# Three pairs by seven products for six units of the conv branch, in a decoder step on one core

## The chip, the cores and the metric

The kernel runs on one core of a Trainium2 chip. The metric is the time of the device in microseconds, median of several runs; lower is better. All matrix work is on TensorE in fp32r, with each operand split into a rounded part and its remainder, so that one product of fp32 accuracy is three matmuls (high by high, high by low, low by high).

## The reference

One layer of a decoder step over 1056 tokens (1024 of a prompt, 8 x 4 samples) of width 1024. The normed input h goes through one wide projection whose columns feed three branches and their gates:

```python
ua, va, q, k, v, cx, cb, cc, ga, gb, gc = split_proj(h, w_in)
out_a = gelu(ua) * spatial_gate(layer_norm(gelu(va)))
out_b = dilated_attention(q, k, v)            # prompt, and samples against a cache
conv, conv_state = short_conv(cc * cx, prev)  # y[t] = b + sum(w[i] * z[t - 2 + i], i = 0..2)
out_c = cb * conv
merged = sig(ga) * (out_a @ w_br_a) + sig(gb) * (out_b @ w_br_b) + sig(gc) * (out_c @ w_br_c)
x = x + rms_norm(merged @ w_o)                # then a SwiGLU block on the normed x
```

The conv branch is 512 wide: four tiles of 128 channels, and for each tile three column groups of w_in (cx, cb, cc), which are three "units".

## The kernel before

Everything lies with channels on the 128 partitions and tokens along the free dimension. A *unit* is 128 output columns of a weight, a tile of 128 x 1024 (eight blocks of 128 inputs). `unit(n)` (L161) takes the next unit of a fixed order written out in `_unit_order` (L47): SyncE's DMA queue loads it (`wr`), ScalarE rounds it (`wh`, L116), VectorE takes the remainder (`wl`, L117). Each of the three tags has three buffers, and one unit is prepared ahead. `fill` (L139) issues other loads on the same queue, behind the last weight load asked for.

**Two ways to multiply.** `proj` (L236) does a unit plainly: three blocks of 352 tokens, 24 matmuls each. `halved` and `seven` (L954, L1003) do two units at once with seven products on half matrices: weights and inputs are cut into halves, sums and differences of the halves are formed on VectorE, and each product is 4 x 3 matmuls of 264 columns for each of two sets of tokens. The first set is the first two quarters of 264 tokens, the second the last two. The differences of the input, kept as high and remainder in `sets`, are made by `halves` (L918) from quarters of h that were spilled to `h_dram`; each half set is four subtractions and four splits of 128 x 1056. `seven` uses four accumulators; with both sets each is a pair of banks (`pair`), with one set a single bank (`psum`).

**Order of the work around the change.** After the prompt's attention come the conv tiles f = 0 to 3 (L1056). For each: two units copied out by ScalarE to z and yb (L1063), a third multiplied into z by VectorE (L1071), in banks of the tag "mm", of which there are two. `conv` (L864) is a generator that then does the three taps on VectorE, multiplies by yb, and spills the result to `outs[6 + f]`. After each block `tick` steps two generators once: the taps of the last tile, and `attn`: the mix of the three dilation groups (L745), the four sample sets (L666, each loading 2.9 MB of masks, keys and values into six tiles, then scores, maximum, exp, transposes and values), and their sum (L812). After f = 2 `attn` is emptied and the first half set is begun; it is stepped during f = 3. Then two gate units are done plainly (L1097), with the second half set beside them, then eleven pairs of gate units by seven products (L1131), each spilled to `sig_dram`. Then the merges (L1167): for j = 0 to 7 three blocks of branch A, multiplied by a gate read back into a tile of V, and three of branch B; `branch_in` (L734) loads and splits the branches' outputs, and the ones of the conv branch come in during the first four steps; after that the merges of C.

Up to the plain gates a planner orders each engine's instructions by their order in the program and by when it thinks them ready; from the gates on (`as_written`, L1096) the matmuls keep the order of the program, and the rest is still planned. Tiles come from pools: 32 tiles of 128 x 1056 called U, of which h takes 16 and the two half sets 16 more, and three of the same size called V, until the merges end.

Of the kernel before, what the change touches and what calls it, by code (L numbers as in the profile page):

```python
# [8 lines left out]
F32 = mybir.dt.float32  # L9
F32R = mybir.dt.float32r  # L10
AF = mybir.ActivationFunctionType
ALU = mybir.AluOpType
AX = mybir.AxisListType

P = 128
# [4 lines left out]
T = TP + TS  # L20
# [25 lines left out]

def _unit_order():  # L47

    n = [(u, False) for u in range(U_G)]
    n[U_UA + 1] = (U_UA + 1, True)  # L50
    n += [(u, False) for u in (U_G, U_G + 1, )]
    n += [(U_BA, False), (U_BB, False), (U_BA + 1, False), (U_BA + 2, False), (U_BB + 1, False), (U_BA + 3, False)]
    n += [(u, False) for u in range(U_BC, U_BC + 4)]
    n += [(U_O + f, f >= REFETCH) for f in range(KD)]
    n += [(U_O + f, False) for f in range(REFETCH)] * 3
    return n
# [3 lines left out]
def tile_decoder_step(ctx: ExitStack, tc: tile.TileContext, i, o):  # L60
    nc = tc.nc
# [16 lines left out]
    def U(dt=F32, w=T):  # L78
        return up.tile([P, w], dt, tag="U", name=nm("U"))

    def V(dt=F32):

        return vp.tile([P, T], dt, tag="V", name=nm("V"))
# [4 lines left out]
    def psum(tag=None):  # L88

        if tag is None:  # L90
            turn[0] += 1
            tag = ("mm", "s", "s")[turn[0] % 3]
        return pp.tile([P, 512], F32, tag=tag, name=nm(tag), bufs=banks[tag])
# [13 lines left out]
    def tmp(tag="ta"):  # L107
        return small([P, 2 * QW], tag, 3)
# [46 lines left out]
    def ahead(n):  # L155
        while len(ready) < n and fetched[0] < len(order):
            m, spare = order[fetched[0]]
            ready.append((m, fetch(m, spare)))
            fetched[0] += 1

    def unit(n, more=1):  # L161

        ahead(1 + more)
        m, halves = ready.pop(0)
        assert m == n, (m, n)
        return halves

    def bs(b):
        return slice(b * BW, (b + 1) * BW)
# [564 lines left out]
    def branch_in(o0, nk, xs):  # L734

        ts = [U() for _ in range(nk)]
        for k, t in enumerate(ts):
            fill(t, outs[o0 + k])
        for t in ts:
            yield  # L740
            xs.append((U(F32R), U(F32R)))
            split(t, *xs[-1])
# [118 lines left out]
    cst = const("cst", [P, 4, 8, 2], i["cst"])  # L861
    convo = const("convo", [P, 4, 18])

    def conv(f, z, yb):  # L864

        zs = small([P, 8, 6], "zs")
        nc.vector.tensor_copy(zs[:, :, 0:2], cst[:, f])
        nc.vector.tensor_copy(zs[:, :, 2:6], z[:, TP:].rearrange("p (b t) -> p b t", t=4))
        nc.vector.tensor_copy(convo[:, f, 0:2], z[:, TP - 2 : TP])
        nc.vector.tensor_copy(convo[:, f, 2:18].rearrange("p (b t) -> p b t", t=2), zs[:, :, 4:6])  # L870
        yield
        y = V()
        cw = [vec(V_CW + 3 * f + t) for t in range(3)]
        cb_ = vec(V_CB + f)
        nc.vector.tensor_scalar(
            out=y[:, :TP], in0=z[:, :TP], scalar1=cw[2], scalar2=cb_, op0=ALU.mult, op1=ALU.add
        )
        ys = y[:, TP:].rearrange("p (b t) -> p b t", t=4)
        nc.vector.tensor_scalar(
            out=ys, in0=zs[:, :, 2:6], scalar1=cw[2], scalar2=cb_, op0=ALU.mult, op1=ALU.add  # L880
        )
        for s in (1, 2):
            nc.vector.scalar_tensor_tensor(
                out=y[:, s:TP], in0=z[:, : TP - s], scalar=cw[2 - s], in1=y[:, s:TP], op0=ALU.mult, op1=ALU.add
            )
            nc.vector.scalar_tensor_tensor(
                out=ys, in0=zs[:, :, 2 - s : 6 - s], scalar=cw[2 - s], in1=ys, op0=ALU.mult, op1=ALU.add
            )
            yield
        nc.vector.tensor_mul(y, y, yb)  # L890
        nc.scalar.dma_start(out=outs[6 + f], in_=y)
        if f == 3:
            nc.scalar.dma_start(out=o["conv"], in_=convo)
        yield

    attn = chain(mix_groups(), *(sample_set(se) for se in range(4)), sample_sum())
    taps = iter(())

    def tick():

        next(taps, None)
        next(attn, None)

# [12 lines left out]
    def halves(s, b11, b21, b12, b22):  # L918


        def sub(out, a, b):
            nc.vector.tensor_tensor(out=out, in0=a, in1=b, op=ALU.subtract)

        sub(b12, b12, b11)
        sub(b22, b22, b12)
        yield
        sub(b11, b22, b11)
        sub(b21, b21, b22)
        put(2, b22, s)
        yield  # L930
        put(3, b11, s)
        put(4, b12, s)
        yield
        put(5, b21, s)
        yield
# [10 lines left out]
    def pair():  # L946
        return pf.tile([P, 1024], F32, tag="pair", name=nm("pair"), bufs=4)
# [6 lines left out]
    def halved(n0, n1, spare):  # L954
# [29 lines left out]
        parts(6, r0[:, b], t, b)  # L984
        return out

    def banks_for(ss):
        return psum() if len(ss) == 1 else pair()

    def product(ps, w, n, ss, start=True):  # L990
        for e, s in enumerate(ss):
# [5 lines left out]
    def by_set(x, ss):  # L997

        return x.rearrange("p (s h t) -> p s h t", s=2, h=2)[:, ss[0] : ss[0] + len(ss)]
# [41 lines left out]
    def left(gen):  # L1041
        for _ in gen:
            pass

    def quarters(s):

        ts = []
        for q in (2 * s, 2 * s + 1):
            for c in range(2):
                t = (V if q == 2 and c else U)()  # L1050
                fill(t.rearrange("p (f t) -> p f t", f=4), h_dram[:, 4 * c : 4 * c + 4, qs_(q)])
                ts.append(t)
        return ts

    others = iter(())
    for f in range(4):  # L1056
        z, yb = U(), U()
        for q, dst in enumerate((z, yb)):
            w = unit(U_C + 3 * f + q)
            for b in range(NB):  # L1060
                ps = psum("mm")
                proj(w, b, ps)
                nc.scalar.copy(dst[:, bs(b)], ps[:, :BW])  # L1063
                tick()
                if f == 3:
                    next(others, None)
        w = unit(U_C + 3 * f + 2)
        for b in range(NB):
            ps = psum("mm")
            proj(w, b, ps)  # L1070
            nc.vector.tensor_tensor(out=z[:, bs(b)], in0=ps[:, :BW], in1=z[:, bs(b)], op=ALU.mult)  # L1071
            tick()
        left(taps)
        taps = conv(f, z, yb)
        if f == 2:
            left(attn)
            others = halves(0, *quarters(0))
    left(others)


    sig_dram = dp.tile([24, P, T], F32, tag="sig_dram", name="sig_dram")
# [13 lines left out]

    as_written[0] = True  # L1096
    for u in range(2):  # L1097
        sig, w = V(), unit(U_G + u)
        for b in range(NB):
            ps = psum()  # L1100
            proj(w, b, ps)
            sigmoid(sig[:, bs(b)], ps[:, :BW], u)
            if u == 0 and b == 0:
                left(taps)
                others = halves(1, *quarters(1))
            next(others, None)
        nc.scalar.dma_start(out=sig_dram[u], in_=sig)
    left(others)
    banked.close()
    mid = ExitStack()  # L1110
# [2 lines left out]
    def gates(w, u, ss, a0, a1):  # L1113
        v0, v1 = by_set(a0, ss), by_set(a1, ss)

        def add(out, ps, u2, u):
            nc.vector.tensor_tensor(out=out, in0=ps, in1=u2, op=ALU.add)
            sigmoid(out, out, u)

        def c22(t):  # L1120
            if t is not None:
                sigmoid(t, t, u + 1)
            return v1[:, :, 1]

        seven(
            w, ss, lambda ps: sigmoid(v0[:, :, 0], ps, u), c22,
            lambda ps, u2: add(v1[:, :, 0], ps, u2, u + 1),
            lambda ps, u2, t: add(v0[:, :, 1], ps, u2, u),
        )

    for u in range(2, 24, 2):  # L1131
        w = halved(U_G + u, U_G + u + 1, V)
# [16 lines left out]
    def merge(j, ts, sig, w, xs, first=False):  # L1149
        ps = psum()[:, : ts.stop - ts.start]  # L1150
        nk = len(xs)
        for k in range(nk):
            c = ((j % (KD // nk)) * nk + k) * P
            mm3(
                ps, (w[0][:, c : c + P], w[1][:, c : c + P]), (xs[k][0][:, ts], xs[k][1][:, ts]),
                k == 0, k == nk - 1,
            )
        dst, s = mg[j][:, ts], sig[:, ts]
        nc.vector.tensor_tensor(out=dst if first else s, in0=ps, in1=s, op=ALU.mult)
        if not first:  # L1160
            nc.vector.tensor_add(dst, dst, s)  # L1161

    xs_a, xs_b, xs_c = [], [], []
    coming = chain(branch_in(0, 4, xs_a), branch_in(4, 2, xs_b), branch_in(6, 4, xs_c))
    for _ in range(7):
        next(coming)
    for j in range(KD):  # L1167
        sig_a, sig_b = gated(j), gated(16 + j)
        if j % 2 == 0:
            wa = unit(U_BA + j // 2)  # L1170
        if j % 4 == 0:
            wb = unit(U_BB + j // 4)
        mg.append(U())
        for b in range(NB):
            merge(j, bs(b), sig_a, wa, xs_a, True)
        for b in range(NB):
            merge(j, bs(b), sig_b, wb, xs_b)
        next(coming, None)
    left(coming)

# [576 lines left out]
```

## Time and profile before

| | |
|---|---|
| median of 3 runs | 1662.18 us (1660.44 to 1662.22) |
| the profiled execution | 1661.68 us, its span 1660.0 us |
| TensorE matmul / weight load busy | 98% / 95% |
| VectorE / ScalarE busy | 62% / 37% |
| mean granted TensorE clock | 0.995 |
| DMA | 221 MB, 133 GB/s over the span |

Times in the rows below are microseconds from the span's start. A matmul's own duration overlaps its neighbours'; what one costs is read from the length of a run of them in the chain of work that ended last.

### The profile page before, as it was taken

What the parts mean: (1) busy time and instruction counts of PE and PEld (TensorE: products, weight loads), DVE (VectorE), ACT (ScalarE), POOL (GpSimd) and SP (SyncE); (2) the same over time, 40 slices, a digit from 0 to 9 for tenths busy, and PEclk for the clock granted to TensorE, in tenths of its full rate; (3) what the DMA queues carried; (4) which work ended last, traced back from release to release, by engine and by line L of the source; (5) the groups of instructions that cost most, each with busy time, mean ns of one, the idle gap of its engine ahead of it and who ended that gap; (6) DMA issues with size and microseconds to landing.
All of it is one profiled execution on the core that took longest, in us unless ns stands there. A gap on an engine that the chain in (4) does not pass through costs nothing.

```text
span 1660.0 us, 29423 instructions
## 1 busy us (share of the span) xinstructions
PE 1624.3 (98%) x12307; PEld 1572.3 (95%) x12307; DVE 1026.4 (62%) x1825; ACT 612.5 (37%) x1129; POOL 12.2 (1%) x23
## 2 busy tenths in 40 slices
PE   7999999999999999999999899999999999999997
PEld 6999887889899999999999899999999999999996
DVE  7536545563374445567776977666666667667586
ACT  7322234411133333341256663322232223344262
POOL 0000100000000000000000000000000000000000
PEclk9999999999999999999999999999999999999998
DMA  6332212033632222276464513333333336746571
GB/s 222 134 108 83 94 45 71 20 137 135 239 109 87 111 108 111 107 268 193 153 206 131 163 46 116 98 98 98 97 98 98 97 97 224 254 169 229 171 251 54
DMA packets 102684, 221.11 MB, mean 133 GB/s; under 512 B 13228, under 2 KB 59884, under 8 KB 102552
## 3 DMA queue, kind: packets, MB, share of 16 engines
q1 hardware_dynamic: 58256, 161.80, 29.5%
q10 hardware_dynamic: 44296, 57.44, 9.8%
q8 instruction: 96, 1.57, 0.4%
q14 instruction: 36, 0.29, 0.1%
HBM read 160.74 MB, written 58.47 MB: 132 GB/s over the span
## 4 chain that ended last, share of the span: by engine, by line
PE 91%; DVE 4%; DMA 2%; issue 1%; ACT 1%; SPq 0%; DVEq 0%
PE pair L123 36%; PE mm L123 19%; PE bank L123 13%; PE s L123 11%; PE s L603 2%; PE t L636 1%; PE o L581 1%; PE s L382 1%; PE s L384 1%; PE s L383 1%; DMA wr<-in_w 1%; DVE wl L117 1%; PE mm L382 1%; PE mm L384 1%; PE mm L383 1%
## 5 line engine op out<-in xcount | busy, mean ns | idle before, releaser
L123 PE MATMUL pair<-U,wh 128*128 128x264 f32 x2880 | 526.6, 284 | 1.6 <-DVE ta L1015 1.6
L123 PEld LDWEIGHTS pair<-U,wh 128*128 128x128 f32 x2880 | 445.7, 188 | 1.8 <-DVE ta L1015 1.8
L123 PE MATMUL pair<-U,wl 128*128 128x264 f32 x1440 | 408.4, 284 | 0.0
L116 ACT CAST wh<-wr 128x512 fp32r<-128x512 f32 (+1 forms) x264 | 192.3, 738 | 441.8 <-PE mm L123 164.7
L123 PE MATMUL mm<-U,wh 128*128 128x352 f32 (+1 forms) x1280 | 314.8, 325 | 2.7 <-ACT U L1063 2.0
L123 PEld LDWEIGHTS pair<-U,wl 128*128 128x128 f32 x1440 | 270.8, 188 | 0.0
L117 DVE TENSOR_TENSOR wl<-wr,wh 128x512 fp32r<-128x512 f32 (+1 forms) x264 | 216.5, 834 | 69.3 <-ACT wh L116 68.6
L123 PEld LDWEIGHTS mm<-U,wh 128*128 128x128 f32 x1280 | 219.5, 188 | 15.5 <-issue 8.8
L123 PE MATMUL bank<-U,wh 128*128 128x264 f32 x1232 | 226.2, 285 | 0.7 <-DVE U L1297 0.7
L123 PE MATMUL mm<-U,wl 128*128 128x352 f32 (+1 forms) x656 | 209.6, 320 | 0.0
L123 PE MATMUL s<-U,wh 128*128 128x352 f32 (+1 forms) x888 | 198.1, 310 | 8.0 <-ACT U L264 5.3
L123 PEld LDWEIGHTS bank<-U,wh 128*128 128x128 f32 x1232 | 191.2, 188 | 1.2 <-DVE U L1297 0.9
L123 PE MATMUL bank<-U,wl 128*128 128x264 f32 x616 | 175.1, 284 | 0.0
L123 PEld LDWEIGHTS s<-U,wh 128*128 128x128 f32 x888 | 149.1, 189 | 10.8 <-ACT U L264 5.3
L123 PE MATMUL s<-U,wl 128*128 128x352 f32 (+1 forms) x460 | 141.3, 307 | 0.0
L117 DVE TENSOR_TENSOR U<-U,U 128x1056 fp32r<-128x1056 f32 (+2 forms) x131 | 113.2, 886 | 23.6 <-ACT U L116 23.1
L123 PEld LDWEIGHTS mm<-U,wl 128*128 128x128 f32 x656 | 123.2, 188 | 1.7 <-issue 1.3
L116 ACT CAST U<-U 128x1056 fp32r<-128x1056 f32 (+2 forms) x131 | 100.1, 781 | 62.5 <-DVE U L1161 28.4
L123 PEld LDWEIGHTS bank<-U,wl 128*128 128x128 f32 x616 | 116.0, 188 | 0.0
L1015 DVE TENSOR_TENSOR tb<-pair,ta 128x528 f32<-128x528 f32 x49 | 34.7, 708 | 108.8 <-PE pair L123 108.8
L123 PEld LDWEIGHTS s<-U,wl 128*128 128x128 f32 x460 | 87.0, 189 | 0.0
L123 PE MATMUL pair<-U,U 128*128 128x264 f32 x456 | 58.5, 284 | 0.0
(291 smaller groups left out, 1863.4 us busy)
## 6 DMA issues: line engine op xcount, KB each, us to landing
wr<-in_w SPq DMA_DIRECT2D x121, 512.0 KB, 4.0
t_dram<-U ACTq DMA_DIRECT2D x77, 264.0 KB, 3.9
U<-t_dram SPq DMA_DIRECT2D x35, 528.0 KB, 5.8
sig_dram<-V ACTq DMA_DIRECT2D x24, 528.0 KB, 2.7
V<-sig_dram SPq DMA_DIRECT2D x24, 528.0 KB, 3.6
U<-in_kv SPq DMA_DIRECT2D x20, 512.0 KB, 6.7
wr<-in_wd SPq DMA_DIRECT2D x20, 512.0 KB, 4.3
U<-outs SPq DMA_DIRECT2D x10, 528.0 KB, 6.6
```

Of the source, the lines that this page charges most:

```text
L116: nc.scalar.copy(hi, x)
L117: (eng or nc.vector).tensor_tensor(out=lo, in0=x, in1=hi.bitcast(F32), op=ALU.subtract)
L123: ins = nc.tensor.matmul(*a, **k)
L382: nc.tensor.matmul(ps[:, :HV], h_hi[k][:, tk], wv[k][0], start=k == 0, stop=False)
L383: nc.tensor.matmul(ps[:, :HV], h_hi[k][:, tk], wv[k][1], start=False, stop=False)
L384: nc.tensor.matmul(ps[:, :HV], h_lo[k][:, tk], wv[k][0], start=False, stop=k == KD - 1)
L581: nc.tensor.matmul(po[0][h * 64 : (h + 1) * 64, (n % 4) * P : (n % 4 + 1) * P], vg[kb // 4][:, (kb % 4) * 256 + hd : (kb % 4) * 256 + hd + ...
L603: nc.tensor.matmul(ps, qT[hs_, n * P : (n + 1) * P], kg[hp][hs_, k0 : k0 + nk * P], start=True, stop=True,)
L636: last = nc.tensor.transpose(tp[:, at : at + P], pt[:, h, c * P : (c + 1) * P], ident)
L1015: nc.vector.tensor_tensor(out=out, in0=view(ps), in1=y, op=ALU.add)
```

## The change

Of the twelve conv units six stay plain: tiles f = 0 and 1. The generators of the attention are stepped three times per block for the first eight blocks and twice after. When the two tiles are done `attn` is emptied, and both half sets are stepped beside the two plain gates, together with the taps of tile 1. Then, before the eleven pairs of the gates, the six units of tiles 2 and 3 are done as three pairs by seven products: the first (cx of both tiles) with one set at a time but in pairs of banks, kept in two V tiles z; the second (cc) multiplied onto z as it comes out; the third (cb) into two V tiles yb. z and yb are spilled to a new `conv_dram`. In the merges' first steps `conv_late` reads them back to U tiles and does the taps of tiles 2 and 3, with the result in a U tile, and the second half of the conv branch's outputs is loaded four steps later than before. The first unit of branch A's weight is now prepared after the first pair and not before it.

```diff
@@ -46,7 +46,7 @@
 
 def _unit_order():
 
-    n = [(u, False) for u in range(U_G)]
+    n = [(u, False) for u in range(U_C + 6)]
     n[U_UA + 1] = (U_UA + 1, True)
     n += [(u, False) for u in (U_G, U_G + 1, )]
     n += [(U_BA, False), (U_BB, False), (U_BA + 1, False), (U_BA + 2, False), (U_BB + 1, False), (U_BA + 3, False)]
@@ -861,7 +861,7 @@
     cst = const("cst", [P, 4, 8, 2], i["cst"])
     convo = const("convo", [P, 4, 18])
 
-    def conv(f, z, yb):
+    def conv(f, z, yb, room):
 
         zs = small([P, 8, 6], "zs")
         nc.vector.tensor_copy(zs[:, :, 0:2], cst[:, f])
@@ -869,7 +869,7 @@
         nc.vector.tensor_copy(convo[:, f, 0:2], z[:, TP - 2 : TP])
         nc.vector.tensor_copy(convo[:, f, 2:18].rearrange("p (b t) -> p b t", t=2), zs[:, :, 4:6])
         yield
-        y = V()
+        y = room()
         cw = [vec(V_CW + 3 * f + t) for t in range(3)]
         cb_ = vec(V_CB + f)
         nc.vector.tensor_scalar(
@@ -896,10 +896,14 @@
     attn = chain(mix_groups(), *(sample_set(se) for se in range(4)), sample_sum())
     taps = iter(())
 
+    ticks = [0]
+
     def tick():
 
         next(taps, None)
-        next(attn, None)
+        ticks[0] += 1
+        for _ in range(3 if ticks[0] < 9 else 2):
+            next(attn, None)
 
 
 
@@ -984,8 +988,10 @@
         parts(6, r0[:, b], t, b)
         return out
 
+    paired = [False]
+
     def banks_for(ss):
-        return psum() if len(ss) == 1 else pair()
+        return psum() if len(ss) == 1 and not paired[0] else pair()
 
     def product(ps, w, n, ss, start=True):
         for e, s in enumerate(ss):
@@ -1052,8 +1058,10 @@
                 ts.append(t)
         return ts
 
-    others = iter(())
-    for f in range(4):
+    def second():
+        yield from halves(1, *quarters(1))
+
+    for f in range(2):
         z, yb = U(), U()
         for q, dst in enumerate((z, yb)):
             w = unit(U_C + 3 * f + q)
@@ -1062,8 +1070,6 @@
                 proj(w, b, ps)
                 nc.scalar.copy(dst[:, bs(b)], ps[:, :BW])
                 tick()
-                if f == 3:
-                    next(others, None)
         w = unit(U_C + 3 * f + 2)
         for b in range(NB):
             ps = psum("mm")
@@ -1071,11 +1077,9 @@
             nc.vector.tensor_tensor(out=z[:, bs(b)], in0=ps[:, :BW], in1=z[:, bs(b)], op=ALU.mult)
             tick()
         left(taps)
-        taps = conv(f, z, yb)
-        if f == 2:
-            left(attn)
-            others = halves(0, *quarters(0))
-    left(others)
+        taps = conv(f, z, yb, V)
+    left(attn)
+    others = chain(halves(0, *quarters(0)), second())
 
 
     sig_dram = dp.tile([24, P, T], F32, tag="sig_dram", name="sig_dram")
@@ -1095,16 +1099,17 @@
 
     as_written[0] = True
     for u in range(2):
-        sig, w = V(), unit(U_G + u)
+        sig, w = V(), unit(U_G + u, 1 - u)
         for b in range(NB):
             ps = psum()
             proj(w, b, ps)
             sigmoid(sig[:, bs(b)], ps[:, :BW], u)
-            if u == 0 and b == 0:
-                left(taps)
-                others = halves(1, *quarters(1))
+            left(taps)
             next(others, None)
+            if b:
+                next(others, None)
         nc.scalar.dma_start(out=sig_dram[u], in_=sig)
+    left(taps)
     left(others)
     banked.close()
     mid = ExitStack()
@@ -1127,6 +1132,57 @@
             lambda ps, u2: add(v1[:, :, 0], ps, u2, u + 1),
             lambda ps, u2, t: add(v0[:, :, 1], ps, u2, u),
         )
+
+    conv_dram = dp.tile([4, P, T], F32, tag="conv_dram", name="conv_dram")
+
+    def plain(w, ss, a0, a1):
+        v0, v1 = by_set(a0, ss), by_set(a1, ss)
+
+        def add(out, ps, u2):
+            nc.vector.tensor_tensor(out=out, in0=ps, in1=u2, op=ALU.add)
+
+        seven(
+            w, ss, lambda ps: nc.scalar.copy(v0[:, :, 0], ps), lambda t: v1[:, :, 1],
+            lambda ps, u2: add(v1[:, :, 0], ps, u2),
+            lambda ps, u2, t: add(v0[:, :, 1], ps, u2),
+        )
+
+    def times(w, ss, a0, a1):
+
+        v0, v1 = by_set(a0, ss), by_set(a1, ss)
+
+        def mult(out, x):
+            nc.vector.tensor_tensor(out=out, in0=x, in1=out, op=ALU.mult)
+
+        def added(out, ps, u2):
+            t = tmp("ta").rearrange("p (s t) -> p s t", s=2)[:, : len(ss)]
+            nc.vector.tensor_tensor(out=t, in0=ps, in1=u2, op=ALU.add)
+            mult(out, t)
+
+        def c12(ps, u2, t22):
+            added(v0[:, :, 1], ps, u2)
+            mult(v1[:, :, 1], t22)
+
+        seven(
+            w, ss, lambda ps: mult(v0[:, :, 0], ps), lambda t: None,
+            lambda ps, u2: added(v1[:, :, 0], ps, u2), c12,
+        )
+
+
+    z = V(), V()
+    w = halved(U_C + 6, U_C + 9, V)
+    paired[0] = True
+    for s in range(2):
+        plain(w, (s,), *z)
+    paired[0] = False
+    ahead(1)
+    times(halved(U_C + 8, U_C + 11, V), (0, 1), *z)
+    yb = V(), V()
+    for k in range(2):
+        nc.scalar.dma_start(out=conv_dram[k], in_=z[k])
+    plain(halved(U_C + 7, U_C + 10, V), (0, 1), *yb)
+    for k in range(2):
+        nc.scalar.dma_start(out=conv_dram[2 + k], in_=yb[k])
 
     for u in range(2, 24, 2):
         w = halved(U_G + u, U_G + u + 1, V)
@@ -1161,7 +1217,18 @@
             nc.vector.tensor_add(dst, dst, s)
 
     xs_a, xs_b, xs_c = [], [], []
-    coming = chain(branch_in(0, 4, xs_a), branch_in(4, 2, xs_b), branch_in(6, 4, xs_c))
+    coming = chain(
+        branch_in(0, 4, xs_a), branch_in(4, 2, xs_b), branch_in(6, 2, xs_c), iter((None,) * 3), branch_in(8, 2, xs_c)
+    )
+
+    def conv_late(k):
+        z, yb = U(), U()
+        fill(z, conv_dram[k])
+        fill(yb, conv_dram[2 + k])
+        yield
+        yield from conv(2 + k, z, yb, U)
+
+    taps = chain(conv_late(0), conv_late(1))
     for _ in range(7):
         next(coming)
     for j in range(KD):
@@ -1173,8 +1240,11 @@
         mg.append(U())
         for b in range(NB):
             merge(j, bs(b), sig_a, wa, xs_a, True)
+            next(taps, None)
         for b in range(NB):
             merge(j, bs(b), sig_b, wb, xs_b)
+        if j == 3:
+            left(taps)
         next(coming, None)
     left(coming)
 
```

## Rows read from the trace of the kernel before

**Rows 1.** The page's first part: busy time, share of the span and instructions of each engine.

```profile
PE 1624.3 (98%) x12307; PEld 1572.3 (95%) x12307; DVE 1026.4 (62%) x1825; ACT 612.5 (37%) x1129; POOL 12.2 (1%) x23
```

**Rows 2.** TensorE's waits from 322 to 735: line, releaser, us in total, times, longest.

```profile
PE mm L123 <- ACT U L1063: 2.0, 1, 2.0
```

**Rows 3.** The chain that ended last, from 444 to 470: start, us, what.

```profile
444.84 0.98 PE s L682 x4
...
455.39 0.20 PE t L816
...
457.03 0.31 ACT ta L831
457.34 0.34 ACT U L1063
...
463.13 6.98 PE mm L123 x43
```

**Rows 4.** The same chain over the span, the longest pieces of the stages touched.

```profile
322.34 9.92 PE mm L123 x60
...
364.34 15.67 PE mm L123 x96
...
486.57 7.74 PE s L123 x48
...
509.81 224.98 PE pair L123 x1848
```

**Rows 5.** SyncE's queue from 290 to 530: start, us over which they were issued, line, what.

```profile
349.00 10.86 SPq L142 DMA_DIRECT2D U<-in_kv  x5
```

**Rows 6.** DMA issues from 321 to 510: line, KB each, median us from issue to landing.

```profile
U<-in_kv SPq DMA_DIRECT2D x20, 512.0 KB, 6.7
...
U<-in_maskS SPq DMA_DIRECT2D x4, 336.0 KB, 3.9
...
sig_dram<-V ACTq DMA_DIRECT2D x1, 528.0 KB, 2.7
```

**Rows 7.** Windows: us, busy of PE, PEld, DVE, ACT, POOL, granted clock, DMA share, GB/s.

```profile
418.70:445.00 26.30, 26.30 (x220) 24.40 (x218) 8.71 (x21) 4.38 (x8) 0.00 (x0) 1.00 0.61 234
...
455.00:458.00 3.00, 0.98 (x16) 0.49 (x13) 1.75 (x11) 1.24 (x4) 0.00 (x0) 1.00 1.08 365
...
470.00:510.00 40.00, 40.00 (x250) 40.00 (x249) 24.12 (x31) 13.14 (x18) 0.00 (x0) 1.00 0.24 82
```

**Rows 8.** VectorE in order of time: taps of tile 2, half sets, weights of a pair.

```profile
441.01 0.81 DVE L875 TENSOR_SCALAR V<-U,vecs 128x1024 f32<-128x1024 f32 x1
...
443.77 1.26 DVE L883 SCALAR_TENSOR_TENSOR V<-U,vecs,V 128x1022 f32<-128x1022 f32 x1
...
446.26 1.24 DVE L890 TENSOR_TENSOR V<-V,U 128x1056 f32<-128x1056 f32 x1
...
459.54 1.26 DVE L922 TENSOR_TENSOR U<-U,U 128x1056 f32<-128x1056 f32 x1
...
465.39 1.25 DVE L117 TENSOR_TENSOR U<-U,U 128x1056 fp32r<-128x1056 f32 x1
...
503.83 0.69 DVE L117 TENSOR_TENSOR V<-tb,V 128x512 fp32r<-128x512 f32 x1
```

**Rows 9.** ScalarE after the second plain gate: a cast, and the write of its sigmoid.

```profile
510.67 0.61 ACT L116 CAST wh<-wr 128x512 fp32r<-128x512 f32 x1
510.80 0.33 ACTq L1107 DMA_DIRECT2D sig_dram<-V  x1
```

**Rows 10.** Windows at the start of the merges, columns as in rows 7.

```profile
717.00:735.00 18.00, 18.00 (x150) 18.00 (x149) 12.49 (x14) 11.08 (x14) 0.00 (x0) 1.00 0.98 369
...
744.00:752.00 8.00, 8.00 (x52) 8.00 (x51) 7.06 (x13) 2.93 (x3) 0.00 (x0) 1.00 0.86 279
752.00:761.00 9.00, 9.00 (x58) 9.00 (x57) 6.97 (x14) 0.07 (x1) 0.00 (x0) 1.00 0.71 218
```

**Rows 11.** VectorE at the first merge of branch B.

```profile
744.83 0.53 DVE L1159 TENSOR_TENSOR V<-s,V 128x352 f32<-128x352 f32 x1 [3.71 <-DMA V<-sig_dram]
```

## The prediction

> **What bounds the kernel now.** I read the page's busy shares first, then the chain of work that ended last, then TensorE's own waits, then the stages that the change touches. TensorE is busy for 1624.3 of 1660.0 us [rows 1], and in the stretch that the change edits the chain runs almost wholly through it. The only wait there that TensorE is charged with is one of 2.0 us [rows 2], ending at 457.7, where an evacuation of a projection bank stands on ScalarE behind the Exp of the sample sums, which waits for VectorE [rows 3]. So a matmul taken away there is time taken away, if what fed TensorE still keeps up, and that is the question.
>
> **The arithmetic, step by step.** A unit is 24 matmuls in each of three blocks, 72 of 352 columns. Beside nothing else 48 take 7.74 us, 161.3 ns each; beside the attention's loads 96 take 15.67 us, 163.2 ns [rows 4]. Six units are 432 matmuls: 69.7 us by the one, 70.5 by the other. A pair by seven products is 7 x 4 x 3 x 2 = 168 matmuls of 264 columns; the eleven pairs of the gates, 1848 matmuls, take 224.98 us without a gap, 121.7 ns each, 20.45 us a pair [rows 4]. Three pairs are 61.4 us. The difference is 8.3 to 9.2 us; I take 8.5, as half of the six units had no attention beside them. The attention's own matmuls move and stay as many.
> The two rates are 2.9 ns plus 0.45 ns per column, so columns decide here and the count hardly does. The Trainium skill (TensorE: Matmul & The Clock Gate, Back-to-back issue gap) gives columns over 2.4 GHz plus 2.5 ns for a lone stream, which would be 149.2 and 112.5 ns and an estimated 7.8 us saved in all; the rows are 8% above both, and the sum goes by them.
>
> **Attention in 18 ticks.** The mix of the groups, the four sample sets and their sum are stepped once per projection block, through three of the four tiles, and then emptied. Now they are stepped three times (from the ninth block, twice) over two tiles, and their 35 steps are out by block 14. Neither the emission nor the room was all that held them: set 0's loads were issued from 349.00 to 359.86, as tiles of the mix came free [rows 5], and that depends on VectorE's mix. So I start set 0's scores at 362, not at 380, where the run of 96 ends [rows 4]. One set, pressed together, took from 444.84 to 455.39, 10.5 us, when the rest was emptied [rows 3]. Its loads are 5 x 0.512 + 0.336 = 2.9 MB: 7.9 us at 365 GB/s, where all DMA engines were busy, 12.4 us at the 234 GB/s of the stretch from 418.7 [rows 6, 7]. With room for two sets of tiles the period is 10.5 to 12.4 us, and set 3 ends at 362 + 3 x that + 10.5 = 404 to 410. The conv stage ran from 322.3 to 486.6 [rows 4], 164.3 us; less 69.7 it ends at 417 (one idle stretch of 2.0 us in it). The attention fits, by 7 to 13 us, and the sum's chain (455.4 to 463.1, 7.7 us) [rows 3] about fits in that. What is new is that every set now has ScalarE's Exp, waiting for VectorE, among the evacuations of only two projection banks. Bounds: 2.0 us gained (the old wait goes) to 6.0 lost (four such waits for one). I take 1.0 lost, near the old single wait, since three of the four sets passed before without any.
>
> **The operands of the pairs.** Before, the first half set was prepared during the fourth conv tile and the second during the two plain gates. Now both stand between the attention's end and the first pair, beside two plain gates of 11.6 us [rows 4]. On VectorE a half set is four subtractions of 1.25 us and four remainders of 1.25 us; two are 20.1 us. The taps of tile 1 are 0.81 + 1.26 + 1.26 + 1.24 and some 1.2 us of small pieces, 5.8 us. The first pair's weights are seven remainders of 0.69 us and five sums of the same size, 8.3 us [rows 8]; the second gate's remainder is 1.2 us, and the adds of set 0 some 3 us. That is 38 us. The last operand of set 1 is due late, since the first pair is run one set at a time: two gates, set 0 (10.2 us) and five of the seven products of set 1 (7.3 us), 23.2 + 10.2 + 7.3 = 40.7 us after the first gate starts. VectorE was 60% busy here before (24.1 of 40 us from 470) [rows 7] and would now be 90% busy. Some of it goes ahead of the gates: before, the first subtraction ran 4 us after the last set's matmuls (459.54 against 455.39) [rows 3, 8], which now gives 408 to 414, ahead of 417. Idle time here: from 0 to the 7 us that come of landing 10 us later (worked out under the second rival); I take 1.5.
> The pool V has three buffers, and z takes two; the third is the split weight of the fifth product, due 5.8 us after the first pair starts. It gets the slot of the second gate's sigmoid, whose write is issued 1.0 us after the last gate matmul and lands 2.7 us later, or of the last quarter; a cast of 0.61 and a remainder of 0.69 follow [rows 6, 8, 9], 5.0 in all: hidden by 0.8 us, and what is behind the waiting cast on ScalarE is the first copy of set 0's product, at 1.5 us. It is the thinnest cover; if it fails it is inside the 7. In the third pair the same slot waits for z's write (2 us of VectorE, two writes, 6 us in all) against 11.7 us: hidden.
> The pair that multiplies has nine VectorE operations where a gate pair has five, some 0.7 us each (0.69 for 512 columns [rows 8], here 528); with 8.3 us of weights that is 14.6 of 20.45 us, no wait. The pairs keep the gates' rhythm of banks and weight slots: nothing.
>
> **The merges.** Tiles 2 and 3 are written (four writes of 0.53 MB from ScalarE's queue), read back by SP, tapped on VectorE and spilled. At the crowded start, from 717 to 735, DMA engines are 98% busy [rows 10]; but two loads of `outs` leave that place (two of four come later), and the first tile's two loads take theirs. VectorE was busy for 14.0 of 17 us [rows 10], so 28.7 of the 34.8 us of the first four steps (a step is 3 x (12 + 6) matmuls at 161.3 ns, 8.7 us); it gets 5.8 us a tile more and loses two splits of 1.25: 37.8, and it falls 3 us behind. The multiply of 744.83 waited 3.71 us for its gate [rows 11] and no matmul waited, as six banks lie between. Ends: 0 and 4 us (that wait again, with the banks full); I take 0. The late pair of `outs` is asked for at step 4, needed 35 us later: hidden.
>
> **Sum.** -8.5 + 1.0 + 1.5 + 0 = -6.0. The profiled execution took 1661.68 us, 0.5 under the median of 1662.18; the span and what lies around it shrink alike, so the median becomes 1656.2.
>
> **The rivals.**
> First, *no new wait*: the conv stage's old one goes and the rest is hidden: 1662.2 - 8.5 - 2 = 1651.7, 1653.7 if it stays. For it: VectorE has the 2.7 us to spare in the sum above, and the gates' pairs never waited. Chance 0.2.
> Second, *the attention's tail and the half sets*, on the slower side. If set 0's quarters land at time L after the first gate starts, 20.1 + 8.3 + 1.2 + 3 us of VectorE follow (the taps done meanwhile), 32.6, so set 1 is late from L = 8 us on, or from 2 us on if the taps are not done; each us later is a us of TensorE's. Landing 13 us later than I reckon (425 instead of 412, so 8 us after 417) costs 0 to 6. To lose the 8.5 and 3.3 more, it must land 14 to 20 us after the first gate starts, at 431 to 437; that is a period of some 18 us a set. It was never asked for here, but with the sets six blocks apart, some 25 us, DMA was at 0.61 [rows 7]; at 12 us apart they and a unit's weights (0.5 MB) are 285 GB/s of the 365. Time: 1666 to 1669. Chance 0.12.
> Third, *half of it*: the same place costs 5 to 10 us and the time lands within 0.2%: 1659 to 1664. Chance 0.2.
> Fourth, *the count of matmuls decides*: 504 for 432 at one price would add 72 x 161.3 ns = 11.6 us: 1673.8. The rows speak plainly against it (0.45 ns per column). Chance 0.01. The same section of the Trainium skill has sustained figures, 81 ns at 128 columns and 131 at 512; drawn straight between them, an estimate, three pairs would come 2 us dearer than six units. The gates' 1848 matmuls at 121.7 ns do not agree with it.
>
> **How the numbers follow.** The forecast, 1654.5 to 1658.8, has 0.47. A measurement tells 0.2%, 3.3 us, from no change, so faster means below 1658.9: 0.47 + 0.2 = 0.67; same 0.2; slower 0.13 (the second and the fourth). The range: below, the saving of 9.2 with the old wait gone, 1651.0; above, it takes in most of the third and stops short of the second: 1665.0.
>
> **What would show it.** Right: from the first plain gate to the last gate pair 14 pairs at 20.45 us each with no gap, the conv stage about 95 us long, 504 more matmuls of 264 columns and 432 fewer of 352, and less than 4 us of new waits. Wrong: scores that wait for `in_kv`, projections that wait for ScalarE's copies, products of the first pair that wait for a remainder of a half set or for the split sum in V, and merges that wait for VectorE. If TensorE's waits stay as they are and the time does not fall, the rate of the pairs was misread.

## The result

The changed kernel takes 1665.09 us (median of 20 runs, 1661.24 to 1667.83), the kernel before, run beside it, 1660.54 us (20 runs). The ratio is 1.0024, 95% interval 1.0017 to 1.0030: slower by 0.24%, where 0.36% faster was forecast. What was forecast to be saved on TensorE was saved; rather more than that was lost in the conv stage, most of it to TensorE's clock.

The profiled execution took 1664.06 us, its span is 1662.1 us. From its page, TensorE's busy time and the clock granted in 40 equal slices (before, every slice but the last read 9, and the last 8):

```profile
PE 1628.1 (98%) x12379; PEld 1567.9 (94%) x12379; DVE 1047.2 (63%) x1870; ACT 616.7 (37%) x1139; POOL 12.2 (1%) x23
...
PEclk9999999979999999999999999999999999999998
```

The shares of busy time are those of [rows 1] to within 1%. The ninth slice of the clock, from 332 to 374, is what differs. The chain that ended last gives the lengths of the stages (start, us, what):

```profile
426.95 7.73 PE s L123 x48
...
450.18 280.30 PE pair L123 x2304
730.56 6.07 PE pair L123 x48
736.63 3.88 PE s L123 x24
```

This answers [rows 4]. Fourteen pairs are 286.4 us, 20.46 each, as 20.45 was forecast. The two plain gates are 23.2 us. The merges run from 736.63, as close together as before. What is longer is the stage in front. In the table the conv stage runs from the start of the prompt's last value matmul to the start of the first pair, less the 23.2 us of the two plain gates. A delay of the gates so counts in it. The pairs run from their first start to the first merge. Starts and chain differ by up to 0.2 us. Each ratio is to runs of the kernel before taken beside that kernel (medians 1660.54, 1660.98 and 1661.13); the experiments have 4 to 11 runs each.

| kernel | conv stage, us | pairs, us | median, us | ratio to before (95%) |
|---|---|---|---|---|
| before | 164.4 | 225.1 (11) | 1660.54 | |
| changed | 106.0 | 286.6 (14) | 1665.09 | 1.0024 (1.0017 to 1.0030) |
| e1_before_mix3 | 167.8 | 225.2 (11) | 1662.47 | 1.0013 (1.0004 to 1.0021) |
| e2_mix1 | 94.1 | 288.4 | 1653.85 | 0.9959 (0.9946 to 0.9971) |
| e3_rows128 | 96.9 | 286.8 | 1652.62 | 0.9952 (0.9939 to 0.9966) |
| e4_one_step | 115.3 | 287.9 | 1675.10 | 1.0086 (1.0072 to 1.0100) |
| e5_both | 90.9 | 288.2 | 1652.32 | 0.9949 (0.9937 to 0.9962) |
| e6_pad12 | 106.2 | 287.1 | 1665.20 | 1.0024 (1.0015 to 1.0034) |
| e7_sets_together | 90.9 | 287.2 | 1651.93 | 0.9942 (0.9930 to 0.9955) |
| e8_two_steps | 90.8 | 288.4 | 1653.06 | 0.9955 (0.9942 to 0.9969) |

By the prediction the stage should have been 164.4 - 69.7 + 1.0 = 95.7 us; it is 106.0. Windows of the changed kernel around the mix of the groups (us, busy time of PE, PEld, DVE, ACT, POOL, granted clock, DMA share, GB/s):

```profile
337.00:338.00 1.00, 1.00 (x5) 0.38 (x3) 1.00 (x3) 0.00 (x0) 0.00 (x0) 1.00 0.11 41
338.00:355.00 17.00, 17.00 (x41) 10.87 (x42) 12.76 (x17) 0.45 (x1) 0.00 (x0) 0.50 0.39 124
355.00:367.00 12.00, 12.00 (x120) 8.90 (x119) 3.98 (x10) 2.71 (x5) 0.00 (x0) 1.00 0.57 206
```

and of the kernel before, the same 17 us:

```profile
338.00:355.00 17.00, 17.00 (x93) 14.61 (x92) 11.27 (x15) 1.40 (x2) 0.00 (x0) 1.00 0.34 112
```

Busy time is 17.00 of 17.00 in both. But in the changed kernel TensorE ran at the lower of its two levels, 1.2 GHz for 2.4, and did 41 matmuls instead of 93 (of a somewhat different mix). The view of waits doesn't show this, since nothing waits. Nor was TensorE idle ahead of it: it was busy for 16.86 of the 17 us from 321 to 338, as before (16.87). In order of time on TensorE, changed kernel (start, us, line, what):

```profile
335.14 2.84 PE L789 MATMUL s<-U,U 12*128 12x512 f32 x10
337.91 0.56 PE L123 MATMUL mm<-U,wl 128*128 128x352 f32 x1
338.40 1.22 PE L789 MATMUL s<-U,U 12*128 12x512 f32 x2
339.55 0.95 PE L123 MATMUL mm<-U,wh 128*128 128x352 f32 x2
```

and before:

```profile
337.21 1.20 PE L789 MATMUL s<-U,U 12*128 12x512 f32 x4
...
342.44 1.19 PE L789 MATMUL s<-U,U 12*128 12x512 f32 x4
```

L789 spreads the softmax weights of the groups over 128 partitions: a matmul of 512 columns with 12 rows of operands out of 128. Before, four of them stood between runs of 24 projections. Stepped three times a block, ten come in a row, and then two between every one to five projections. Two that take 0.62 us at full clock take 1.22.

The second loss in the stage is at the scores of the sample sets. Chain of the changed kernel:

```profile
355.79 0.98 PE s L682 x4
...
357.61 0.98 PE s L682 x4
```

and of the kernel before:

```profile
380.01 0.99 PE s L682 x8
```

A set has four such score matmuls, which the trace records as eight. Each writes 32 of the 128 output rows, and eight records in one run take as long as four. So a run that is cut in two costs 2 x 0.98 - 0.99 = 0.97 us more. In the changed kernel the planner cut the runs of all four sets, with projections between; before, it cut one of four. That is three cuts more, 2.9 us, or 1.9 if the last set is left out: the second half of its run also waited for its load (from the order of time):

```profile
397.72 1.05 PE L682 MATMUL s<-U,qs 128*32 128x512 f32 x4 [0.63 <-DMA U<-in_kv]
```

TensorE's waits from 321 to 735:

```profile
PE s L682 <- DMA U<-in_kv: 0.6, 1, 0.6
PE s L686 <- DMA U<-in_kv: 0.2, 1, 0.2
```

These 0.8 us are all; the 2.0 us of [rows 2] are gone.

### The profile page after: what moved, and what is told of

Its sections match the earlier page's. It is cut to its first block, busy times and chain, and to the rows that moved or that the text cites. A ratio compares the mean times of both kernels' runs of the same rounds, so it can differ in the third digit from the quotient of the medians.

```text
span 1662.1 us, 29667 instructions
## 1 busy us (share of the span) xinstructions
PE 1628.1 (98%) x12379; PEld 1567.9 (94%) x12379; DVE 1047.2 (63%) x1870; ACT 616.7 (37%) x1139; POOL 12.2 (1%) x23
## 4 chain that ended last, share of the span: by engine, by line
PE 87%; DVE 6%; DMA 2%; issue 2%; ACT 2%; DVEq 0%; SPq 0%; ACTq 0%
PE pair L123 39%; PE mm L123 15%; PE bank L123 11%; PE s L123 11%; PE s L603 2%; PE t L636 1%; PE o L581 1%; DVE wl L117 1%; DVE U L117 1%; PE s L382 1%; PE s L384 1%; PE s L383 1%; DMA t_dram<-U 1%; PE s L789 1%; DMA U<-in_kv 1%
## 5 line engine op out<-in xcount | busy, mean ns | idle before, releaser
L123 PE MATMUL pair<-U,wh 128*128 128x264 f32 x3168 | 578.7, 284 | 0.8 <-DVE ta L1021 0.7
L123 PEld LDWEIGHTS pair<-U,wh 128*128 128x128 f32 x3168 | 490.4, 188 | 1.1 <-DVE ta L1021 0.9
L123 PE MATMUL pair<-U,wl 128*128 128x264 f32 x1584 | 449.4, 284 | 0.0
L123 PEld LDWEIGHTS pair<-U,wl 128*128 128x128 f32 x1584 | 298.2, 188 | 0.0
L123 PE MATMUL mm<-U,wh 128*128 128x352 f32 (+1 forms) x992 | 248.8, 328 | 0.7 <-ACT wh L116 0.7
L123 PEld LDWEIGHTS mm<-U,wh 128*128 128x128 f32 x992 | 172.4, 191 | 15.1 <-issue 10.4
L123 PE MATMUL mm<-U,wl 128*128 128x352 f32 (+1 forms) x512 | 166.0, 324 | 0.0
L123 PEld LDWEIGHTS s<-U,wh 128*128 128x128 f32 x888 | 150.5, 191 | 10.4 <-ACT U L264 5.9
L1021 DVE TENSOR_TENSOR tb<-pair,ta 128x528 f32<-128x528 f32 (+1 forms) x54 | 37.7, 698 | 120.1 <-PE pair L123 120.1
L123 PEld LDWEIGHTS mm<-U,wl 128*128 128x128 f32 x512 | 97.5, 190 | 5.9 <-issue 5.6
L1021 DVE TENSOR_TENSOR ta<-pair,tb 128x528 f32<-128x528 f32 (+1 forms) x34 | 23.4, 689 | 59.0 <-PE pair L123 59.0
```

The lines of the kernel that those rows point to most:

```text
L123: ins = nc.tensor.matmul(*a, **k)
L1021: nc.vector.tensor_tensor(out=out, in0=view(ps), in1=y, op=ALU.add)
```

## The experiments

Theory A: the run of 12-row matmuls lets the clock fall. Theory B: the attention as a whole is too dense for half the blocks (loads, scores, evacuations). The prediction had only B. The two don't exclude each other: the runs ask how much is A's.

**One part alone, in the kernel before.** The mix is stepped as the change steps it, all else stays.

```diff
+    ticks = [0]
     def tick():
         next(taps, None)
-        next(attn, None)
+        ticks[0] += 1
+        for _ in range(3 if ticks[0] < 3 else 1):
+            next(attn, None)
```

> The kernel before with one part of the change alone: the attention is stepped three times per block in the first two blocks (which puts out the whole mix of the groups) and once per block after that. If the clock is the cause (theory A: the mix's matmuls, which use 12 of 128 rows, come ten in a row and TensorE's granted clock falls to 0.5 for some 17 us from there), this kernel loses 7 to 9 us against before, about 1668, and shows a stretch at 0.5 near 340. If it is the density of the whole attention (theory B: loads, scores and evacuations of four sets in half the blocks), the sets stand here as before and the time is within 2 us of before, with the clock at 1.0.

1662.47 us, ratio 1.0013 (1.0004 to 1.0021). The window of its mix:

```profile
338.00:355.00 17.00, 17.00 (x51) 12.44 (x51) 10.30 (x15) 1.49 (x3) 0.00 (x0) 0.60 0.35 124
```

The clock falls, without any conv pair in the kernel, so stepping alone brings it. The time, within 2 us of before, is what was expected of B; it is the clock that speaks for A. The conv stage is 3.4 us longer than before, not 8. The low stretch is shorter (13.7 us, 6.9 us of work lost), the old wait of 2.0 us is gone, and so is the one cut in the scores (0.97 us), which leaves 3.9. In the median only 1.5 us are left. In the profiled executions the stages behind the pairs are 3.0 us shorter than before (922.3 us for 925.3). The kernel before has two short stretches at 0.5 there, near 894 and 952, 6.8 us together, and this execution has none. What brings those was not tested.

**The mix spread out again, in the changed kernel.**

```diff
-        for _ in range(3 if ticks[0] < 9 else 2):
+        for _ in range(1 if ticks[0] < 7 else 3):
```

> The changed kernel with the attention stepped once per block for the first six blocks (the mix) and three times after. Theory A: no run of the mix's matmuls, clock at 1.0 through the conv stage, 8 us faster than the changed kernel: about 1657, 0.2% faster than before. Theory B: the four sets are pressed into fewer blocks still, so no gain on the changed kernel or a loss: 1665 to 1668.

1653.85 us, ratio 0.9959 (0.9946 to 0.9971). Its window:

```profile
338.00:355.00 17.00, 16.77 (x81) 14.49 (x81) 12.73 (x18) 1.40 (x2) 0.00 (x0) 0.90 0.40 131
```

One short stretch at 0.5 is left (3.4 us), behind a run of ten that starts at 347.06. The sets now stand in fewer blocks than in the changed kernel, which B held to be worse, and the stage is 94.1 us. B alone falls. But the 11.2 us won are more than the 8 expected, and not all of them are the clock's: three of the four sets' scores stand undivided here, and none waits for its load.

**The same run of matmuls over 128 rows.** Order and number stay; the operands get rows of zeros.

```diff
-        sel12 = U(F32R)[:12, : 6 * P]
-        nc.vector.tensor_copy(sel12, sel_raw)
+        sel12 = U(F32R)[:, : 6 * P]
+        nc.gpsimd.memset(sel12.bitcast(F32), 0.0)
+        nc.vector.tensor_copy(sel12[:12], sel_raw)
...
-        rT = U(F32R, TP)[:12], U(F32R, TP)[:12]
+        rT = U(F32R, TP), U(F32R, TP)
+        for t in rT:
+            nc.gpsimd.memset(t.bitcast(F32), 0.0)
...
-            split(tp[:12], rT[0][:, cols], rT[1][:, cols])
+            split(tp[:12], rT[0][:12, cols], rT[1][:12, cols])
```

> The changed kernel with the mix's matmuls in the same order and number, over 128 rows instead of 12 (the added rows of both operands are zero). Theory A in the form that the rows in use count: the clock stays at 1.0 and the time falls by 7 to 9 us, to about 1657. Theory A in another form (the kind of matmul or the run itself, whatever its rows, or that zeros do not count): the clock falls to 0.5 as before, 1665. Theory B: 1665.

1652.62 us, ratio 0.9952 (0.9939 to 0.9966). The run of ten and the window:

```profile
335.59 2.84 PE L792 MATMUL s<-U,U 128*128 128x512 f32 x10
```

```profile
338.00:355.00 17.00, 16.33 (x98) 12.54 (x98) 15.33 (x24) 2.90 (x5) 0.00 (x0) 1.00 0.53 170
```

The run is as long as in the changed kernel, the clock stays at its upper level, and the median is 12.5 us lower. That is more than the 7 to 9 expected. In the conv stage it is 9.1 us. The changed kernel's trace also has two short stretches at 0.5 behind the pairs, near 952 and 1017, 6.8 us together, and this one has none; how often either kernel has them is not known.

**The control:** the same tiles, zeros and order, but the matmuls read 12 rows.

```diff
-                            sel12[:, (g * 2 + hp) * P : (g * 2 + hp + 1) * P],
-                            rT[q][:, half * 512 : (half + 1) * 512],
+                            sel12[:12, (g * 2 + hp) * P : (g * 2 + hp + 1) * P],
+                            rT[q][:12, half * 512 : (half + 1) * 512],
```

> A control for e3_rows128: the same tiles, fills with zeros and order, but the mix's matmuls read 12 rows again. If the rows in use are what counted, the clock falls to 0.5 for 14 to 20 us near 340 and the time is that of the changed kernel, about 1665. If the fills or a shifted order had mended it, the clock stays at 1.0 and the time is that of e3_rows128, about 1653.

1665.20 us, ratio 1.0024 (1.0015 to 1.0034), the changed kernel's time again. Its run of ten and its window:

```profile
335.60 2.85 PE L792 MATMUL s<-U,U 12*128 12x512 f32 x10
```

```profile
338.00:355.00 17.00, 17.00 (x45) 10.94 (x45) 13.15 (x18) 0.45 (x1) 0.00 (x0) 0.56 0.38 124
```

So the fills and the slots did nothing; the rows that the matmuls read of both operands decide, and 9.3 us of the conv stage (106.2 to 96.9) hang on them.

**The attention at one step per block throughout.**

```diff
-        for _ in range(3 if ticks[0] < 9 else 2):
+        for _ in range(1):
```

> The changed kernel with the attention stepped once per block throughout, so that half of it (sets 1 to 3 and the sum) is emptied when the two conv tiles are done. Theory A: the clock stays at 1.0 in the mix, which gives 8 us back, but three sets of 10.5 us and the sum then have hardly a projection between them and the half sets wait for them: 20 to 30 us of idle TensorE, 1677 to 1687. Theory B (density costs, the tail is hidden under the two gates): 1653 to 1657.

1675.10 us, ratio 1.0086 (1.0072 to 1.0100). TensorE's waits from 315 to 470, the longest:

```profile
PE t L709 <- ACT U L702: 8.1, 3, 3.5
PE t L844 <- DVE ta L841: 3.5, 1, 3.5
PE t L712 <- DVE U L710: 2.4, 3, 0.8
```

and its window when the projections are used up:

```profile
400.00:437.00 37.00, 21.06 (x246) 13.52 (x239) 17.39 (x55) 5.52 (x14) 0.00 (x0) 0.66 0.42 141
```

Three sets without projections between them leave TensorE idle for 16 of 37 us, somewhat less than expected, and with TensorE idle the clock fell too. In the mix, which stands here as before, it stayed at 1.00. So the attention has to be stepped faster than before; it is the mix that must not be.

**Both mends.** The edits of e2_mix1 and e3_rows128.

> The changed kernel with both mends: the mix stepped once per block for six blocks (three steps after), and its matmuls over 128 rows. Theory A (rows in use hold the clock): no stretch at 0.5 before the output projection, where e2_mix1 still had one of 3.4 us; 0 to 1.7 us faster than e2_mix1, 1652 to 1654. If the two mends were separate gains, each 8 us and more from causes other than the clock, they would add up: 1645 to 1648.

1652.32 us, ratio 0.9949 (0.9937 to 0.9962): 8.8 us faster than before. No low stretch in the mix:

```profile
338.00:355.00 17.00, 16.77 (x96) 15.42 (x95) 13.53 (x19) 1.40 (x2) 0.00 (x0) 1.00 0.43 141
```

They don't add up, as A says of two mends for one cause. The conv stage is 90.9 us. Against e3_rows128, where the clock was mended too, the stage is 6.0 us shorter. About 4.2 of that can be named: one set's scores are cut here against four there (2.9 us), no set waits for its loads (0.9 us there), and a wait in the mix is 0.2 us for 0.6. The median shows little of it (1652.62 against 1652.32, intervals that overlap). The trace of this kernel has two short stretches at 0.5, near 884 and 942, where that of e3_rows128 has none, which hides some of it; how much stays is open.

**The first pair.** Its only waits in e5_both, and its ScalarE in order of time (the first pair starts at 435.7):

```profile
PE pair L123 <- ACT ta L1029: 1.0, 1, 1.0
PE pair L123 <- DVE ta L1024: 0.4, 1, 0.4
```

```profile
436.39 1.06 ACT L116 CAST U<-U 128x1056 fp32r<-128x1056 f32 x1
436.52 0.32 ACTq L1114 DMA_DIRECT2D sig_dram<-V  x1
437.36 1.07 ACT L116 CAST U<-V 128x1056 fp32r<-128x1056 f32 x1
438.33 1.14 ACT L116 CAST wh<-wr 128x512 fp32r<-128x512 f32 x2
439.37 0.37 ACT L1029 COPY ta<-pair 128x264 f32<-128x264 f32 x1
```

Two casts of the last half set and two of weights stand ahead of the first product's copy. Two kernels try this, both from e5_both. One steps the half sets twice in every block of the gates:

```diff
-            if b:
-                next(others, None)
+            next(others, None)
```

> e5_both with the half sets stepped twice in every block of the plain gates (once in the first block of each before). If the 1.0 us wait of the first pair in e2_mix1 comes of the last half set's casts standing ahead of the first copy on ScalarE, it goes: 1 us faster than e5_both. If it comes of the third tile of V (the split weight behind the gate's write), it stays.

1653.06 us, ratio 0.9955 (0.9942 to 0.9969), with the same wait of 1.0 us. By the expectation that points to the third tile of V. The rows say otherwise: ScalarE is busy without a gap from 436.39 to the copy, so no cast there waits for a tile. Its order is the same in both kernels, so this edit changed nothing and doesn't decide. That the planner sets the casts by when it thinks them ready would explain it, and was not tested. The other does both sets of the first pair at once:

```diff
-    paired[0] = True
-    for s in range(2):
-        plain(w, (s,), *z)
-    paired[0] = False
+    plain(w, (0, 1), *z)
```

> e5_both with the first pair done for both sets at once, so that set 1's operands are due 10 us earlier. By the prediction's count (38 us of VectorE for 40.7, of which 10.2 came of the one-set order) TensorE waits 5 to 8 us in the first pair: 1658 to 1660. If VectorE's work lies further ahead than counted, no more than the 1 us that e2_mix1 waits there: 1652 to 1654.

1651.93 us, ratio 0.9942 (0.9930 to 0.9955), not to be told from e5_both. TensorE's waits in its pairs:

```profile
PE pair L123 <- DVE ta L1024: 0.5, 1, 0.5
```

The wait for the copy goes, as the second product now lasts twice as long, and no wait for the half sets comes. So the operands were ready earlier than the prediction's count had them. The test is milder than its expectation says: only the first operands of set 1 are due 7 to 9 us earlier. The last is due after five of seven products either way, 14.6 us into the pair for 17.5, so 3 us earlier.

## Why the prediction was wrong

**The arithmetic** was right: three more pairs at 20.46 us each, and two rates that follow the columns. With both mends the change gives 8.8 us (e5_both), where 8.5 were forecast ahead of the waits. That they agree is in part luck: conv stage and pairs together are 10.4 us shorter there, of which 2.0 are the old wait that is gone. The fourth rival (the count of matmuls decides) falls.

**Attention in 18 ticks** is the step that failed. It asked whether loads, tiles and evacuations keep up, bounded the cost by waits (2.0 us gained to 6.0 lost) and took 1.0 lost; 11.3 was measured. It didn't ask what the denser order does to TensorE itself. The stage came out 11.3 us over 164.4 - 69.7: 17 us at half the clock are 8.5 us (9.3 by e3_rows128 against e6_pad12); scores cut in two 1.9 to 2.9; waits for loads 0.8; the old wait's 2.0 gone; 0.3 to 2.1 us are not attributed. Its dates were about right: the sets' scores started at 355.8 (362 forecast), and the first subtraction of the half sets ran at 411.3 (408 to 414 forecast):

```profile
411.30 1.24 DVE L926 TENSOR_TENSOR U<-U,U 128x1056 f32<-128x1056 f32 x1
...
445.82 1.25 DVE L117 TENSOR_TENSOR U<-V,U 128x1056 fp32r<-128x1056 f32 x1
```

The prediction took the idle time of TensorE to be all that could be lost. The clock of 1.00 in [rows 7] could not tell it otherwise: those windows lie behind the mix, and the order before had at most four of the mix's matmuls between 24 projections. The row to ask about was one not read, the shape 12x512 of L789, though nothing in the trace of before shows what a run of such matmuls does.
The Trainium skill (TensorE: Matmul & The Clock Gate, HAM oscillation — how this bites in real kernels) has the clock fall over idle gaps of TensorE. This trace shows a fall without one: it came at 338 with TensorE busy for 16.86 of the 17 us before and 17.00 of the 17 after. What the runs show is that matmuls over few rows, busy as they look, don't hold it.

**The operands of the pairs**: 1.5 us of idle time forecast, none found in the pairs of the changed kernel (286.6 us against 14 x 20.45 = 286.3), 1.4 in e5_both, where the stage ahead is shorter. The count of 38 us of 40.7 was too tight: the last remainder of the half sets, the second row above, was done at 447.1, 20.3 us after the first gate started. All subtractions of the first half set had run by 417.7, ahead of the gates. e7_sets_together, with less time, has no wait for the half sets either. The cover called the thinnest, the copy behind a cast on ScalarE, is the one that showed, but by casts in the queue and not by a slot of V.

**The merges** cost nothing, as forecast: the first 109.8 us of them (736.63 to 846.43) took 109.6 before.

**The rivals**: the second named the right side and the wrong mechanism; nothing landed late. What it feared, an attention whose tail comes late, is what e4_one_step shows: 1675.10 us. None of the rivals had the clock, so the chance of 0.13 for slower came from a case that didn't happen.

## What to carry to other kernels

When small matmuls are moved closer together between large ones, look at the rows of their operands, not only at their time: a denser stretch of matmuls over few rows can lower the clock for all that stands among them, and waits and busy time don't show it, only the granted clock and a matmul's own duration. Here, filling the operands up with zeros to all rows cost no time on TensorE (2.84 us for the run of ten either way) and kept the clock. Spreading them between full ones kept it but for 3.4 us. A saving by fewer columns is sound, but work that hid beside the removed matmuls must be given a new place, and its order there is part of the price.

## What the runs showed of the hardware

- Ten matmuls in a row of 512 columns with 12 rows in use were followed by a fall of the granted clock to 0.5. It stayed there for 17 us, in which two of them stood between every one to five full ones, with TensorE busy throughout. With 128 rows in use, 116 of them zero, the same order ran at 1.00: rows of zeros held the clock as well. How few rows it takes, and which operand's rows count, was not tested.
- The matmuls that write 32 of 128 output rows took 0.98 us for a run of four records and 0.99 us for a run of eight.
- The mean granted clock of the changed kernel's runs went from 0.988 to 0.992 and their times from 1667.83 to 1661.24 us, by and large the lower the clock the longer. Whether the stretch of the mix or the short ones behind it differ is not known, since one execution has a trace.
